# A state-space core worked by feature chunk, four pairs of groups side by side in TensorE's array, in place of pair by pair with zero padding

## The chip, the cores and the metric

The kernel runs on one core of a Trainium2 chip. The metric is the device time of one execution in microseconds. A core has TensorE (matrix products, with a queue of its own for weight loads), VectorE, ScalarE, GpSimd and SyncE (which issues the DMAs); in profile rows they are PE and PEld, DVE, ACT, POOL and SP. They run side by side, each in the order of its own queue, and wait for one another by semaphores.

## The reference

The reference is a stack of layers on a sequence of 256 tokens with 1024 features: in the first block a short convolution, a state-space mixer, an RWKV mixer and another convolution, each followed by a gate and a layer norm; a second block with attention and feed-forward layers follows. The change lies in the state-space mixer:

```python
def s5_mixer(x, w_in, lam_re, lam_im, log_dt, b_re, b_im, c_re, c_im, d_skip, w_glu, b_glu, w_out):
    u, z = jnp.split(x @ w_in, 2, axis=-1)
    ug = u.astype(f32).reshape(bsz, seqlen, SSM_GROUPS, SSM_GROUP)
    ...
    a_bar = jnp.exp(lam * dt)
    b_bar = ((a_bar - 1.0) / lam)[..., None] * b_mat
    bu = jnp.einsum("blgh,gph->blgp", ug, b_bar)
    a_seq = jnp.broadcast_to(a_bar, bu.shape)
    states = lax.associative_scan(_ssm_combine, (a_seq, bu), axis=1)[1]
    y = jnp.einsum("blgp,ghp->blgh", states, c_mat).real + d_skip.astype(f32).reshape(SSM_GROUPS, SSM_GROUP) * ug
    y = jax.nn.gelu(y.reshape(bsz, seqlen, D_INNER).astype(x.dtype))
    y = y * jax.nn.sigmoid(y @ w_glu + b_glu)
    return (y * jax.nn.silu(z)) @ w_out
```

There are 64 groups of 16 features, each with 64 complex states. A chunk is 128 features, so there are 8 chunks of 8 groups.

## The kernel before, in words

Activations lie feature-major: 8 chunks of 128 partitions by 256 tokens. Most weights are split into two halves (`whi` on ScalarE, line 599, `wlo` on VectorE, line 600) and multiplied in three passes; `ssm_in`, the mixer's input projection, is used as plain fp32. An fp32 matmul shows as two rows of the trace.

The order of work is chosen when the program is written out: generators hand out instructions, a planner estimates when each engine is done (`Model`, `Engine`, `TensorE`), and `weave` and `par` emit the generator that can go on first. A side iterator `ada` (the second block's modulation) is woven in at a set pace: per column tile one 512 KB load of `in_ada` and two VectorE products, the `junk` rows of line 1354. The helpers record every operation, so that VectorE and ScalarE instructions have line 402 and matmuls line 431.

`ssm_prep` (818 to 924) makes, during the first layer, the matrices: `bT` for the input product, `ca`, `cm` and `cn` for the output product, `gm` for the direct term of even steps, `rho` and `f2` (size and phase of the recurrence). Two time steps go at a time, so a sequence of 256 becomes two halves of 128. `ple_norm` (778 to 816) ends the first layer with a norm, whose `rsqrt` is a chain of VectorE and ScalarE steps (`tc` rows) before the eight `x` writes from which the projection starts.

`ssm` (926 to 1036): `project` makes the 16 column tiles of the projection (`u` and the gate `sz`). Beside it `pairs(j)` runs for 32 pairs of groups, three at a time. A pair has 32 features and 128 states. Its steps:

- ScalarE copies the pair's 32 rows of `u` into its place in `um`, a buffer that is zero elsewhere;
- the phases: two ScalarE steps, one VectorE step, sine, absolute value, sine, all of 128x128;
- the input product bu: eight 128x128 matmuls (K 128 by way of the zeros) into a `ca` bank;
- VectorE rotates the bank by the phases (`m1`, `m2`, `w`), scans twice along time, and rotates back;
- the output product y: nine matmuls with 32 output columns into 32 rows of a `cb` bank that four pairs share; after the fourth pair VectorE adds the skip term into `y`.

Then come the activation of `y`, the gated product (`ssm_glu`) and `ssm_out`. PSUM banks: three for projections (`mm`), one for sums (`st`), two each of `ca` and `cb`.

Of the kernel before, what the change touches and what calls it, by code (L numbers as in the profile page):

```python
# [86 lines left out]
def constants():  # L87
# [172 lines left out]
# ---------------------------------------------------------------- the program  # L260
# [4 lines left out]
class Stream:  # L265
    """A generator of instructions. It yields a request (array name, block, K chunks, columns) for a weight
    block, which it is sent, or a float where TensorE needs what the other engines have been given to do (Until: a time)."""
# [22 lines left out]
    def keeps(self):  # L290
        """the other stream will want the block too"""
# [29 lines left out]
class Model:  # L321
    """An estimate of when the data of tiles is there, by which the order of instructions is chosen"""
# [29 lines left out]
    def alloc(self, tile, key, bufs):  # L352
        """the tile takes the place of the one `bufs` before it"""
# [7 lines left out]
class Engine:  # L361
    """nc.vector or nc.scalar, with an estimate of when its instructions end: each starts in the first gap that is long
    enough once its operands are there"""
# [17 lines left out]
    def any_time(self, dur):  # L381
        """work whose operands come early"""
# [24 lines left out]
class TensorE:  # L407
    """nc.tensor, with an estimate of the time that its instructions take"""
# [13 lines left out]
    def matmul(self, out, lhsT, rhs, start, stop):  # L422
# [3 lines left out]
        elif m > 64:  # L426
            dur = max(n, 128) / 600.0
# [10 lines left out]
class Net:  # L438
# [45 lines left out]
    def slot(self, i, shape, name, dt=F32):  # L484
        """the i-th of 14 pieces of 8 KB per partition"""
# [9 lines left out]
    def big(self, name):  # L495
        """a piece of 9 KB"""
# [21 lines left out]
    def act(self, out, in_, func, **kw):  # L518
        """an activation; keeps track of the table set that it leaves"""
# [10 lines left out]
    # ---- order of emission  # L530
# [3 lines left out]
    def weave(self, streams, until=None):  # L534
        """emits the streams' instructions, the first that can go on, until the condition or all are done"""
# [51 lines left out]
    # ---- weights: fp32 blocks from DRAM, each split into two float32r parts whose sum it is  # L587
# [22 lines left out]
    def mm3(self, out, w, x, m=0, k0=0, start=True, stop=True):  # L610
        """out += w[:, :, column tile m]^T x[:, k0:] over the K chunks; w, x: (hi, lo) pairs, or float32 both."""
# [14 lines left out]
    def mm3g(self, out, w, x, m=0):  # L626
        """generator: mm3 in pieces, between which others' instructions may go"""
# [1319 lines left out]
```

## Time and profile before

| | us |
|---|---|
| runs | 2926.54, 2930.72, 2931.11 (median 2930.72) |
| span of the profiled execution | 2931.2 |
| PE busy | 2814.3 (96%) |
| DVE busy | 2142.3 (73%) |
| ACT busy | 1631.4 (56%) |
| state-space core, first projection to last y | 185.4 to 357.1 |

The span's row by engine is an average over stages with different limits; the core's own stretch is read by windows, in which busy times of the engines, the granted clock of TensorE (1.00 is 2.4 GHz, 0.50 is 1.2 GHz) and DMA share stand for one stretch. Busy times of PE rows overlap, since matmuls are pipelined; so the distance from start to start is read from rows "xN", which join N like instructions: first start, time from the first start to the last end.

### The profile page before, as it was taken

The page shows a single profiled execution, that of the slowest core. Times are in us where ns is not written, and L with a number is a line of the kernel's source. Part 1 is how long each engine was busy: PE and PEld are TensorE (multiplying, and loading weights), DVE is VectorE, ACT ScalarE, POOL GpSimd, SP SyncE. Part 2 cuts the span into 40 slices and gives each one's busy share as a digit, 9 for nine tenths or more (in the row PEclk, how much of TensorE's full clock was granted, in tenths as well). Part 3 has the DMA queues.
Part 4 walks back from the last instruction along what each step waited for, and adds up shares of the span by engine and source line. Part 5 has one row for each costly group of instructions (what it writes and reads, how often), then busy time and mean ns, then how long its engine had stood idle before and what let it go on. Part 6 is the DMA issues. An engine that isn't in the chain of part 4 may idle for free.

```text
span 2931.2 us, 58792 instructions
## 1 busy us (share of the span) xinstructions
PE 2814.3 (96%) x23798; PEld 2652.5 (90%) x23798; DVE 2142.3 (73%) x4116; ACT 1631.4 (56%) x3069; POOL 16.6 (1%) x42
## 2 busy tenths in 40 slices
PE   8989998899999999999999999999999999999999
PEld 8977788787999999998999978999999999996999
DVE  8876777666678788898898887877855336676655
ACT  5644556766646464778566766544522224466443
POOL 0000000000000000000000000000000000000000
PEclk9989998999999999999999999999999999999999
DMA  7632353200466666666675644666544323221554
GB/s 266 216 130 94 100 185 123 81 23 33 140 213 203 215 201 221 205 194 190 196 224 182 194 155 129 208 223 212 181 144 125 100 82 102 92 87 57 160 182 142
DMA packets 129296, 454.89 MB, mean 155 GB/s; under 512 B 14336, under 2 KB 18688, under 8 KB 128384
## 3 DMA queue, kind: packets, MB, share of 16 engines
q1 hardware_dynamic: 129024, 451.13, 48.3%
q8 instruction: 187, 3.06, 0.4%
q14 instruction: 85, 0.70, 0.1%
HBM read 450.02 MB, written 1.05 MB: 154 GB/s over the span
## 4 chain that ended last, share of the span: by engine, by line
PE 68%; DVE 14%; DMA 8%; ACT 6%; issue 4%; SPq 0%; DVEq 0%; ACTq 0%
PE ps_mm L431 56%; DMA w<-in_ada_dram 7%; PE ps_ca L431 5%; PE ps_cb L431 5%; DVE wlo L600 5%; DVE junk L1354 3%; ACT whi L599 2%; DVE tc L402 1%; PE ps_st L431 1%; PE ps_cb L435 1%; ACT L402 1%; ACT rw_b L402 1%; ACT tc L402 1%; DVE h_lo L402 1%; DMA w<-in_ffn_in_dram 1%
## 5 line engine op out<-in xcount | busy, mean ns | idle before, releaser
L599 ACT ACTIVATE whi<-w 128x1024 fp32r<-128x1024 f32 (+1 forms) x687 | 715.9, 1044 | 731.1 <-PE ps_mm L431 474.1
L600 DVE TENSOR_TENSOR wlo<-w,whi 128x1024 fp32r<-128x1024 f32 (+1 forms) x687 | 826.3, 1204 | 240.7 <-ACT whi L599 238.8
L431 PE MATMUL ps_mm<-h_hi,whi 128*128 128x256 f32 x3024 | 868.0, 289 | 6.1 <-ACT h_hi L402 4.4
L431 PE MATMUL ps_mm<-h_lo,whi 128*128 128x256 f32 x3024 | 856.0, 284 | 2.5 <-DVE h_lo L402 2.4
L431 PE MATMUL ps_mm<-h_hi,wlo 128*128 128x256 f32 x3024 | 853.2, 283 | 3.1 <-DVE wlo L600 3.0
L431 PEld LDWEIGHTS ps_mm<-h_hi,whi 128*128 128x128 f32 x3024 | 569.7, 189 | 15.8 <-ACT h_hi L402 6.3
L431 PEld LDWEIGHTS ps_mm<-h_lo,whi 128*128 128x128 f32 x3024 | 570.2, 189 | 8.7 <-DVE h_lo L402 3.7
L431 PEld LDWEIGHTS ps_mm<-h_hi,wlo 128*128 128x128 f32 x3024 | 570.9, 189 | 7.4 <-DVE wlo L600 4.9
L1354 DVE SCALAR_TENSOR_TENSOR junk<-w,cond 128x1024 bf16<-128x1024 f32 x288 | 351.9, 1222 | 125.9 <-DMA w<-in_ada_dram 124.8
L431 PE MATMUL ps_mm<-d_hi,whi 128*128 128x256 f32 x1232 | 353.4, 287 | 0.9 <-DVE ctx L402 0.4
L431 PE MATMUL ps_mm<-d_hi,wlo 128*128 128x256 f32 x1232 | 348.5, 283 | 3.6 <-DVE wlo L600 3.6
L431 PE MATMUL ps_mm<-d_lo,whi 128*128 128x256 f32 x1232 | 349.6, 284 | 0.0
L431 PEld LDWEIGHTS ps_mm<-d_hi,wlo 128*128 128x128 f32 x1232 | 233.2, 189 | 4.9 <-DVE wlo L600 4.7
L431 PEld LDWEIGHTS ps_mm<-d_hi,whi 128*128 128x128 f32 x1232 | 232.4, 189 | 4.0 <-issue 2.6
L431 PEld LDWEIGHTS ps_mm<-d_lo,whi 128*128 128x128 f32 x1232 | 232.4, 189 | 2.7 <-issue 1.6
L402 DVE TENSOR_TENSOR td<-td,ps_mm 128x256 f32<-128x256 f32 x154 | 64.5, 419 | 82.3 <-PE ps_mm L431 78.8
L402 ACT ACTIVATE d_hi<-td 128x256 fp32r<-128x256 f32 x154 | 63.0, 409 | 79.2 <-DVE td L402 78.4
L402 ACT ACT_TABLE_LOAD x81 | 103.9, 1283 | 2.5 <-PEq L1938 0.7
L431 PE MATMUL ps_mm<-x_hi,whi 128*128 128x256 f32 x256 | 73.6, 287 | 12.4 <-ACT whi L599 12.4
L402 ACT ACTIVATE tc<-tc 128x256 f32<-128x256 f32 x182 | 75.2, 413 | 6.0 <-DVE tc L402 3.1
L402 ACT ACTIVATE td<-ps_mm 128x256 f32<-128x256 f32 x154 | 57.1, 373 | 33.5 <-PE ps_mm L431 33.1
L431 PE MATMUL ps_mm<-xs_hi,whi 128*128 128x256 f32 x256 | 72.7, 284 | 2.7 <-ACT whi L599 1.6
(459 smaller groups left out, 5466.2 us busy)
## 6 DMA issues: line engine op xcount, KB each, us to landing
w<-in_ffn_in_dram SPq DMA_DIRECT2D x268, 512.0 KB, 4.0
w<-in_ada_dram SPq DMA_DIRECT2D x144, 512.0 KB, 4.3
w<-in_ffn_out_dram SPq DMA_DIRECT2D x96, 512.0 KB, 4.1
w<-in_conv_in_dram SPq DMA_DIRECT2D x64, 512.0 KB, 4.5
w<-in_ffn_out_dram SPq DMA_DIRECT2D x48, 384.0 KB, 3.5
w<-in_ab_in_dram SPq DMA_DIRECT2D x34, 512.0 KB, 4.4
w<-in_ple_gate_dram SPq DMA_DIRECT2D x32, 512.0 KB, 4.4
w<-in_conv_out_dram SPq DMA_DIRECT2D x16, 512.0 KB, 4.6
```

What stands on the lines that cost most here:

```text
L402: return f(**kw)
L431: self.t.matmul(out, lhsT=lhsT, rhs=rhs, start=start, stop=stop)
L435: self.t.transpose(out, in_, ident)
L599: nc.scalar.activation(out=hi[:, :n], in_=w[:, :n], func=AF.Copy)
L600: nc.vector.tensor_tensor(out=lo[:, :n], in0=w[:, :n], in1=hi[:, :n].bitcast(F32), op=ALU.subtract)
L1354: nc.vector.scalar_tensor_tensor(out=self.junk, in0=w, scalar=1.0, in1=cb[:, s], op0=ALU.mult, op1=ALU.mult, accum_out=m[:, t, s:s + 1])
```

## The change

The core works by chunk of four pairs, two chunks at a time, each with its own two slots of 8 KB (0 and 1, or 6 and 7).

- bu: instead of 128 rows with zeros, each pair's 32 rows are the contraction, so that four pairs lie in four row quarters of the array; the four results go to four banks (`ca`, `cb`, `ca`, `cb`), from which ScalarE copies them to `w`. `um`, its memset and its 32 copies go; one copy per chunk orders even and odd steps (`uc`).
- y: the four pairs' matmuls with 32 columns each are written next to each other, in four column quarters, into one `st` bank. The direct term's matrix `gm` is now masked to the pairs' blocks (`bd32`, a constant of 128 more columns), by a VectorE multiply in place of the ScalarE copy.
- VectorE and ScalarE steps run over four pairs at once: the phases on 128x512, rotations on 128x1024, sums on 128x512; scans stay 128x128.
- The planner prices such matmuls at a quarter (`share=4`).

```diff
+    c.add("bd32", np.kron(np.eye(4), np.ones((32, 32))))
...
-    def matmul(self, out, lhsT, rhs, start, stop):
+    def matmul(self, out, lhsT, rhs, start, stop, share=1):
...
-        elif m > 64:
-            dur = max(n, 128) / 600.0
+        elif m > 64 or share > 1:
+            dur = max(n, 128) / 600.0 / share
...
-                    A.activation(out=merge(gm[:, 4 * h:4 * h + 4]), in_=ps, func=AF.Copy)
+                    tt(gm[:, 4 * h:4 * h + 4], ps.rearrange("p (c n) -> p c n", c=4), self.c("bd32").unsqueeze(1).to_broadcast([128, 4, 128]), MUL)
...
-        um = self.slot(6, [2, 2, 4, N], "um")
-        nc.gpsimd.memset(um, 0.0)
...
-        sets = [t1_[:, :1024], t1_[:, 1024:], t11[:, 1024:]]
-        free = list(range(3))
+        sets = [tuple(self.slot(k, [2048], f"ssm_m{k}") for k in ks) for ks in ((0, 1), (6, 7))]
+        free = list(range(2))
...
-        def pairs(j):
+        def group(c):
...
-            A.activation(out=uc[rows, :, i], in_=halves(u[rows, c]), func=AF.Copy)
-            v, kk = m2[:, 0], m2[:, 1]
-            A.activation(out=v, in_=tsh, func=AF.Identity, scale=f2[:, j:j + 1])
+            uc = two(self.tmp("ta"))
+            A.activation(out=uc, in_=halves(u[:, c]), func=AF.Copy)
+            for i in range(4):
+                A.activation(out=v[:, i], in_=tsh, func=AF.Identity, scale=f2[:, 4 * c + i:4 * c + i + 1])
             A.activation(out=kk, in_=v, func=AF.Identity, bias=self.fixed[MAGIC])
             V.scalar_tensor_tensor(out=v, in0=kk, scalar=MAGIC, in1=v, op0=SUB, op1=SUB)
-            self.act(cs[:, 1], v, AF.Sin, scale=-TWO_PI)
+            self.act(si, v, AF.Sin, scale=-TWO_PI)
             A.activation(out=v, in_=v, func=AF.Abs)
-            self.act(cs[:, 0], v, AF.Sin, scale=-TWO_PI, bias=half_pi)
+            self.act(co, v, AF.Sin, scale=-TWO_PI, bias=half_pi)
...
-            b = two(self.ps("ca")[:, :S])
+            ps = [self.ps(("ca", "cb")[i % 2])[:, :S] for i in range(4)]
             for q in range(2):
                 for r in range(2):
-                    T.matmul(b[:, q], lhsT=bT[1 - r][:, q, c], rhs=uc[:, r, i], start=r == 0, stop=r == 1)
-            tt(m1, b, co, MUL)
-            tt(m2, b, si, MUL)
...
+                    for i, l in enumerate(lanes):
+                        T.matmul(two(ps[i])[:, q], lhsT=bT[1 - r][l, q, c], rhs=uc[l, r], start=r == 0, stop=r == 1, share=4)
+            for i in range(4):
+                A.activation(out=w[:, i], in_=two(ps[i]), func=AF.Copy)
+            tt(m1, w, both(co), MUL)
+            tt(m2, w, both(si), MUL)
+            tt(w[:, :, 0], m1[:, :, 0], m2[:, :, 1], ADD)
+            tt(w[:, :, 1], m2[:, :, 0], m1[:, :, 1], SUB)
+            for i in range(4):
+                for q in range(2):
+                    x_ = w[:, i, q]
+                    V.tensor_tensor_scan(out=x_, data0=rho[:, 4 * c + i:4 * c + i + 1].to_broadcast([128, N]), data1=x_, initial=0.0, op0=MUL, op1=ADD)
+            tt(m1, w, both(co), MUL)
+            tt(m2, w, both(si), MUL)
             yield 4.0
-            if c not in yps:
-                yps[c] = self.ps("cb")
...
+            yp = two(self.ps("st")[:, :S])
+            for i in range(4):
+                T.matmul(yp[lanes[i], 0], lhsT=gm[:, c, lanes[i]], rhs=uc[:, 0], start=True, stop=False, share=4)
             for r, cc in ((0, ca), (1, cm)):
                 n = N - 1 + r
...
+                for k in range(4):
+                    for i in range(4):
+                        j = 4 * c + i
...
+                        T.matmul(yp[lanes[i], r, N - n:], lhsT=l_, rhs=m_[:, :n], start=r == 1 and k == 0, stop=k == 3, share=4)
             free.append(q_)
...
-        yield from self.par((pairs(j) for j in range(32)), 3, project())
+        yield from self.par((group(c) for c in range(NCH)), 2, project())
```

The change moves instructions on every engine inside the core; before it and behind the start of the gated product the order is the old one. Three places:

ScalarE at the end of the first layer's norm, from the squares (`sq`) to the writes of `x`, before (`tc` are the steps of the inverse root):

```order
L402 ACTIVATE sq<-r 128x256 x8
L393 ACT_TABLE_LOAD
L402 ACTIVATE tc<-ps_st,fixed_64 128x256
L402 ACTIVATE tc<-tc 128x256 x2
L402 ACTIVATE x<-r,pr 128x256 x8
```

The same place after (`ssm_m_2152` and `ssm_m_2153` are the slots of chunk 0: phases, then sine and cosine):

```order
L394 ACT_TABLE_LOAD
L403 ACT_TABLE_LOAD
L403 ACTIVATE ssm_m_2153<-ssm_m_2152 128x512
L403 ACT_TABLE_LOAD
L403 ACTIVATE tc<-ps_st,fixed_64 128x256
L403 ACTIVATE ssm_m_2152<-ssm_m_2152 128x512
L403 ACT_TABLE_LOAD
L403 ACTIVATE tc<-tc 128x256
L403 ACT_TABLE_LOAD
L403 ACTIVATE ssm_m_2153<-ssm_m_2152,fixed_72 128x512
L403 ACTIVATE tc<-tc 128x256
L403 ACTIVATE x<-r,pr 128x256 x8
```

Chunk 0's sine, absolute value and cosine stand among the norm's three steps, with four table loads more. On VectorE at the same place, after, from the last step of the squares' sum to the scaling of `r` (`junk` rows are the modulation's, with the number of their weight tile):

```order
L403 TENSOR_TENSOR sq_2083<-sq_2083 128x256
L1360 SCALAR_TENSOR_TENSOR junk_101,mod_63<-w_2172,cond0_157 128x1024
L403 SCALAR_TENSOR_TENSOR ssm_m0_2152<-ssm_m0_2152 128x512
L1360 SCALAR_TENSOR_TENSOR junk_101,mod_63<-w_2172,cond0_157 128x1024
L1360 SCALAR_TENSOR_TENSOR junk_101,mod_63<-w_2199,cond0_157 128x1024 x2
L403 SCALAR_TENSOR_TENSOR tc_2110<-ps_st_2105,tc_2110 128x256
L1360 SCALAR_TENSOR_TENSOR junk_101,mod_63<-w_2226,cond0_157 128x1024
L403 SCALAR_TENSOR_TENSOR tc_2109<-tc_2110,tc_2109 128x256
L1360 SCALAR_TENSOR_TENSOR junk_101,mod_63<-w_2226,cond0_157 128x1024
L403 SCALAR_TENSOR_TENSOR r_1415<-r_1415,pr_58,tc_2109 128x256 x8
```

Before, two `junk` rows stand there ahead of the first `tc` row, and none between it and `r`.

TensorE inside the core, before (one piece: a part of a projection tile, one pair's y in the column quarter of its rows):

```order
L431 MATMUL ps_mm<-x,w 128x256 x4
L431 MATMUL ps_cb<-um,ssm_s_159 32x128
L431 MATMUL ps_cb<-ssm_s_159,ssm_s_204 32x127 x3
L431 MATMUL ps_cb<-ssm_s_159,cn 32x127
L431 MATMUL ps_cb<-ssm_s_159,ssm_s_203 32x128 x3
L431 MATMUL ps_cb<-ssm_s_159,cn 32x128
```

And after, at chunk 0's y:

```order
L433 MATMUL ps_mm<-x,w 128x256 x20
L433 MATMUL ps_st<-ta,ssm_s_159 32x128 x4
L433 MATMUL ps_st<-ssm_m_2152,ssm_s_204 32x127 x12
L433 MATMUL ps_st<-ssm_m_2152,cn 32x127 x4
L433 MATMUL ps_st<-ssm_m_2152,ssm_s_203 32x128 x12
L433 MATMUL ps_st<-ssm_m_2152,cn 32x128 x4
L433 MATMUL ps_mm<-x,w 128x256 x12
```

A y is now 36 matmuls in one piece, and neighbours in a row lie in different column quarters.

ScalarE between chunks 2 and 3, after (`2152`, `2153` hold chunk 2, `2154`, `2155` chunk 3; `fixed_70` adds the rounding number, `fixed_72` makes the second sine of the phases a cosine):

```order
L403 ACTIVATE ssm_m_2153<-ssm_m_2152,fixed_72 128x512
L403 ACTIVATE u<-ps_mm 128x256
L403 ACTIVATE ta<-u 128x256
L403 ACTIVATE ssm_m_2154<-cond_157,f_161 128x128 x4
L403 ACTIVATE ssm_m_2154<-ssm_m_2154,fixed_70 128x512
L403 ACTIVATE ssm_m_2155<-ssm_m_2154 128x512
L403 ACTIVATE ssm_m_2154<-ssm_m_2154 128x512
L403 ACTIVATE ssm_m_2153<-ps_ca 128x256
L403 ACTIVATE ssm_m_2153<-ps_cb 128x256
```

Chunk 2's evictions from `ps_ca` and `ps_cb` stand behind chunk 3's phases and its first sine; before, nothing was evicted there, since VectorE read the `ca` banks itself.

## Rows read from the trace of the kernel before

**Rows 1.** Stretches: length, busy us (rows) of each engine, clock, DMA.

```profile
core 0: us, PE busy (x) PEld busy (x) DVE busy (x) ACT busy (x) POOL busy (x), PEclk, DMA share, GB/s
173.00:190.00 17.00, 9.05 (x21) 6.23 (x21) 14.42 (x34) 8.97 (x20) 0.00 (x0) 0.50 0.19 62
190.00:344.00 154.00, 152.97 (x1043) 124.00 (x1042) 107.38 (x323) 70.73 (x194) 0.00 (x0) 1.00 0.29 93
347.10:354.00 6.90, 5.60 (x27) 4.50 (x27) 4.82 (x14) 4.24 (x11) 1.82 (x4) 0.51 0.36 112
354.00:430.00 76.00, 76.00 (x628) 75.07 (x627) 57.68 (x100) 43.73 (x82) 2.70 (x6) 1.00 0.59 183
```

**Rows 2.** The chain of waits from 191 to 357 us, by line.

```profile
by line: PE ps_cb L431 38.0%; PE ps_mm L431 35.9%; PE ps_ca L431 19.0%; DMA w<-in_ssm_glu_dram 2.8%; DVE ssm_s L402 1.9%; ACT ssm_s L402 0.8%; issue 0.6%; ACT whi L599 0.6%; DVE y L402 0.3%; DVE mod L402 0.1%; DVE wlo L600 0.0%
```

**Rows 3.** Groups from 191 to 362 us: busy, mean ns | idle, releaser.

```profile
L431 PE MATMUL ps_mm<-x,w 128*128 128x256 f32 x243 | 62.3, 390 | 0.0
L431 PEld LDWEIGHTS ps_cb<-ssm_s,ssm_s 128*32 128x32 f32 x384 | 39.2, 111 | 13.6 <-DVE ssm_s L402 8.1 <-issue 3.0 <-ACT whi L599 0.2
L431 PE MATMUL ps_ca<-um,bT 128*128 128x128 f32 x256 | 37.0, 286 | 1.0 <-DVE ssm_s L402 1.0
L431 PE MATMUL ps_cb<-ssm_s,ssm_s 128*32 128x127 f32 x192 | 30.5, 281 | 4.0 <-DVE ssm_s L402 3.9
...
L1354 DVE SCALAR_TENSOR_TENSOR junk<-w,cond 128x1024 bf16<-128x1024 f32 x20 | 24.3, 1217 | 0.6 <-DMA w<-in_ada_dram 0.6
...
L402 ACT ACTIVATE ssm_s<-ssm_s 128x128 f32<-128x128 f32 x58 | 17.2, 301 | 4.3 <-DVE ssm_s L402 3.5
...
L402 ACT ACTIVATE um<-u 32x256 f32<-32x256 f32 x32 | 13.8, 432 | 2.0 <-PE ps_cb L431 1.3
...
L600 DVE TENSOR_TENSOR wlo<-w,whi 128x1024 fp32r<-128x1024 f32 x4 | 4.8, 1217 | 0.0
...
L402 ACT ACTIVATE u<-ps_mm 128x256 f32<-128x256 f32 x8 | 3.0, 377 | 13.1 <-PE ps_mm L431 13.1
```

**Rows 4.** TensorE's timeline: start us, length us, runs of like matmuls.

```profile
202.13 0.82 PE L431 MATMUL ps_cb<-ssm_s,ssm_s 128*32 128x128 f32 x6
...
207.10 2.05 PE L431 MATMUL ps_ca<-um,bT 128*128 128x128 f32 x16
208.99 5.35 PE L431 MATMUL ps_mm<-x,w 128*128 128x256 f32 x24
```

**Rows 5.** TensorE's timeline in the RWKV heads and the attention.

```profile
587.35 0.68 PE L431 MATMUL ps_cb<-rw_b 128*64 128x64 f32 x14
...
1324.06 1.08 PE L431 MATMUL ps_mm<-pt,kava 128*64 128x256 f32 x8
```

**Rows 6.** VectorE's timeline: runs of like instructions inside the core.

```profile
261.98 0.75 DVE L402 TENSOR_TENSOR ssm_s<-ssm_s 128x256 f32<-128x256 f32 x2
...
263.58 0.74 DVE L402 TENSOR_TENSOR_SCAN ssm_s<-rho,ssm_s 128x128 f32<-128x128 f32 x2
...
341.89 2.36 DVE L600 TENSOR_TENSOR wlo<-w,whi 128x1024 fp32r<-128x1024 f32 x2
```

**Rows 7.** Timeline of the norm's end, all engines.

```profile
179.16 1.28 ACT L393 ACT_TABLE_LOAD   x1
...
183.45 0.42 DVE L402 SCALAR_TENSOR_TENSOR tc<-ps_st,tc 128x256 f32<-128x256 f32 x1 [2.01 <-ACT tc L402]
...
185.45 7.73 PE L431 MATMUL ps_mm<-x,w 128*128 128x256 f32 x24 [3.44 <-ACT x L402]
```

**Rows 8.** Timeline of the core's end, TensorE and VectorE.

```profile
348.40 1.48 PE L431 MATMUL ps_cb<-ssm_s,ssm_s 128*32 128x127 f32 x6 [3.95 <-DVE ssm_s L402]
...
351.94 1.01 PE L431 MATMUL ps_mm<-ys_hi,whi 128*128 128x256 f32 x3
...
356.61 0.48 DVE L402 SCALAR_TENSOR_TENSOR y<-u,pr,ps_cb 128x256 f32<-128x256 f32 x1 [1.23 <-PE ps_cb L431]
```

More of the change, by code (lines that the diff above doesn't have):

```diff
@@ L822, in ssm_prep @@
         N = S // 2
[L823 removed]
+        tsh = self.second[:, 2 * D:2 * D + N + 128]
         self.consts("ssm", tsh)
@@ L960, in ssm @@
             A.activation(out=cn[:, r], in_=cc[:, 1], func=AF.Copy, scale=-1.0)
[L961 to L964 removed]
+        sets = [tuple(self.slot(k, [2048], f"ssm_m{k}") for k in ks) for ks in ((0, 1), (6, 7))]
+        free = list(range(2))
         halves = lambda t: t.rearrange("p (t r) -> p r t", r=2)
         two = lambda t: t.rearrange("p (q t) -> p q t", q=2)
[L968 to L969 removed]
+        lanes = [slice(32 * i, 32 * i + 32) for i in range(4)]
+        def group(c):
             while c not in came:
@@ L972, in pairs @@
             q_ = free.pop(0)
-            m1, m2, cs, w = (two(sets[q_][:, 256 * q:256 * q + 256]) for q in range(4))
-            rows = slice(32 * i, 32 * i + 32)
-            uc = um[:, c % 2]
-            A.activation(out=uc[rows, :, i], in_=halves(u[rows, c]), func=AF.Copy)
-            v, kk = m2[:, 0], m2[:, 1]
-            A.activation(out=v, in_=tsh, func=AF.Identity, scale=f2[:, j:j + 1])
+            a, b = sets[q_]
+            m1, m2, w = (t.rearrange("p (i q t) -> p i q t", i=4, q=2) for t in (a[:, :1024], a[:, 1024:], b[:, :1024]))
@@ L980, in pairs @@
+            co, si = (b[:, 1024 + 512 * k:1536 + 512 * k].rearrange("p (i t) -> p i t", i=4) for k in range(2))
+            v, kk = (a[:, 1024 + 512 * k:1536 + 512 * k].rearrange("p (i t) -> p i t", i=4) for k in range(2))
+            uc = two(self.tmp("ta"))
+            A.activation(out=uc, in_=halves(u[:, c]), func=AF.Copy)
+            for i in range(4):
+                A.activation(out=v[:, i], in_=tsh, func=AF.Identity, scale=f2[:, 4 * c + i:4 * c + i + 1])
             A.activation(out=kk, in_=v, func=AF.Identity, bias=self.fixed[MAGIC])
@@ L981, in pairs @@
             V.scalar_tensor_tensor(out=v, in0=kk, scalar=MAGIC, in1=v, op0=SUB, op1=SUB)
-            self.act(cs[:, 1], v, AF.Sin, scale=-TWO_PI)
+            self.act(si, v, AF.Sin, scale=-TWO_PI)
             A.activation(out=v, in_=v, func=AF.Abs)
-            self.act(cs[:, 0], v, AF.Sin, scale=-TWO_PI, bias=half_pi)
-            co, si = (cs[:, q:q + 1].to_broadcast([128, 2, N]) for q in range(2))
+            self.act(co, v, AF.Sin, scale=-TWO_PI, bias=half_pi)
+            both = lambda t: t.unsqueeze(2).to_broadcast([128, t.shape[1], 2, N])
@@ L986, in pairs @@
             yield 2.0
-            b = two(self.ps("ca")[:, :S])
+            ps = [self.ps(("ca", "cb")[i % 2])[:, :S] for i in range(4)]
             for q in range(2):
                 for r in range(2):
-                    T.matmul(b[:, q], lhsT=bT[1 - r][:, q, c], rhs=uc[:, r, i], start=r == 0, stop=r == 1)
-            tt(m1, b, co, MUL)
-            tt(m2, b, si, MUL)
-            tt(w[:, 0], m1[:, 0], m2[:, 1], ADD)
-            tt(w[:, 1], m2[:, 0], m1[:, 1], SUB)
-            for q in range(2):
-                V.tensor_tensor_scan(out=w[:, q], data0=rho[:, j:j + 1].to_broadcast([128, N]), data1=w[:, q], initial=0.0, op0=MUL, op1=ADD)
@@ L999, in pairs @@
+            for i in range(4):
[4 more added lines that the diff above has]
+            tt(m2, w, both(si), MUL)
             yield 4.0
-            if c not in yps:
-                yps[c] = self.ps("cb")
-            yp = two(yps[c][:, :S])
-            T.matmul(yp[rows, 0], lhsT=gm[:, c, rows], rhs=uc[:, 0, i], start=True, stop=False)
+            yp = two(self.ps("st")[:, :S])
@@ L1004, in pairs @@
+            for i in range(4):
+                T.matmul(yp[lanes[i], 0], lhsT=gm[:, c, lanes[i]], rhs=uc[:, 0], start=True, stop=False, share=4)
             for r, cc in ((0, ca), (1, cm)):
                 n = N - 1 + r
-                for k, (l_, m_) in enumerate(((cc[:, 0, j], m1[:, 0]), (cc[:, 0, j], m2[:, 1]), (cc[:, 1, j], m2[:, 0]), (cn[:, r, j], m1[:, 1]))):
-                    T.matmul(yp[rows, r, N - n:], lhsT=l_, rhs=m_[:, :n], start=r == 1 and k == 0, stop=k == 3)
+                for k in range(4):
+                    for i in range(4):
+                        j = 4 * c + i
+                        l_, m_ = ((cc[:, 0, j], m1[:, i, 0]), (cc[:, 0, j], m2[:, i, 1]), (cc[:, 1, j], m2[:, i, 0]), (cn[:, r, j], m1[:, i, 1]))[k]
+                        T.matmul(yp[lanes[i], r, N - n:], lhsT=l_, rhs=m_[:, :n], start=r == 1 and k == 0, stop=k == 3, share=4)
@@ L1008, in pairs @@
             free.append(q_)
-            left[c] -= 1
-            if left[c] == 0:
-                V.scalar_tensor_tensor(out=halves(y[:, c]), in0=halves(u[:, c]), scalar=self.p("ssm_d", c), in1=two(yps.pop(c)[:, :S]), op0=MUL, op1=ADD)
+            V.scalar_tensor_tensor(out=halves(y[:, c]), in0=halves(u[:, c]), scalar=self.p("ssm_d", c), in1=yp, op0=MUL, op1=ADD)
         self.fine = FINE & 1
-        yield from self.par((pairs(j) for j in range(32)), 3, project())
+        yield from self.par((group(c) for c in range(NCH)), 2, project())
```

8 lines of the change are left out of this document (1 added, 7 removed).

## Prediction

> **What bounds the kernel now.** I read the stretches first, because the order of work differs only between the end of the first layer's norm and the gated product (GLU) behind the state-space core; elsewhere each engine has its old row order, so the forecast is a shift of everything behind the core. From 190 to 344 us TensorE is busy 152.97 of 154 us at the full clock, VectorE 107.38, ScalarE 70.73 [rows 1]; the chain of waits runs over TensorE there (38.0, 35.9 and 19.0%) [rows 2]. TensorE's work falls into three parts, by start-to-start distance in runs of one kind [rows 3, 4]: 256 rows of projection (243 recorded) at (5.35-0.39)/23 = 0.216 us, 55 us; 256 rows of input product (bu) at (2.05-0.29)/15 = 0.117, 30 us (another run gives 0.122); 576 rows of output product (y; six groups of `ps_cb`, the largest shown) at (0.82-0.27)/5 = 0.109, 63 us. That is 148 us, the stage. Two rows make one fp32 matmul.
>
> **The change, part by part.** TensorE keeps its matmul count: a chunk has 32 bu rows and 72 y rows. Before, they cost 32 x 0.122 = 3.9 and 72 x 0.109 = 7.85 us a chunk. Now four neighbours in the order use four different quarters of the array. The trace never shows four. It shows two: 14 rows of 128*64 tiles in 0.68 us (0.068 us each after the first), and eight rows 128x256 in 1.08 us where a row by itself takes 0.216 every time [rows 4, 5]: pairs run nearly as one. From two to four is an extrapolation; bounds for a chunk are 2.0 + 1.0 us (all four as one) and 7.85 + 3.9 (none). I take 2.1 + 1.0, as the rows that are nearest show nearly full overlap, and keep the partial case as a rival. TensorE's need then falls from 148 to 55 + 8 x 3.1 = 80 us, and **another engine sets the end**.
>
> The Trainium skill ("TensorE: Matmul & The Clock Gate", Part 3: Packing small matmuls — row/col tiling) says that a weight load overlaps running matmuls only in another row group, which speaks against the y part, whose four column tiles use all rows. Here the column-tile loads, 111 ns each, hide behind matmuls on the same rows, at 0.109 us a row [rows 3, 4]; by the row y is 2.1 us a chunk, by the rule 36 x 0.111 + 2.1 = 6.1, an estimate, and the sum would be near 2903.
>
> VectorE per chunk: four 128x1024 at 1.14 (2.36-1.22, the split), two 128x512 at 0.65 (twice the 128x256's 0.33), eight scans at 0.33 [rows 6]: 4.6+1.3+2.6 = **8.6 us**, plus y 0.5 and the phase step 0.65. This is hardly less than before: the same elements in fewer instructions.
>
> ScalarE: the 32 copies into the padded buffer (13.8 us) go, one of 128x256 per chunk (0.4) comes; the bu result is now evicted, four of 128x256 at 0.38 per chunk [rows 3]. The phase chain becomes 128x512 at about 0.6 (128x128 0.30, 128x256 0.38, carried on). TensorE hid ScalarE before; now it stands in the path.
>
> *Start of the core.* Chunk 0's sines can only be written once the old tenants of its slots are done, so they fall into the norm's ScalarE chain, where Sin, Ln and Exp alternate: five table loads instead of one, each 1.28 [rows 7]. By the new order: squares end 179.1; two loads to 181.7; sin 182.3; load, Ln 184.1; abs 184.7; load, Exp 186.4; load 187.7; sin 188.3; Square 188.7. VectorE's step after it moves from 183.45 [rows 7] to 188.7. Two modulation products (1.2 each [rows 3]) now stand between it and the x writes: first projection at 185.45 + 5.2 + 2.4 less rounding = **192.9, 7.5 us late**. Then three projection tiles (48 rows) precede bu. The clock was 1.2 GHz until 190.1, 4.65 us after the first matmul [rows 1, 7]; the same again gives 11 rows at 0.43 and 37 at 0.216: 205.6. bu 1.0, and the last evictions: VectorE starts chunk 0 at **207.9**.
>
> *A cycle of two chunks* (two sets of buffers), from the start t of chunk c's block: block c ends t+8.6; block c+1 with one modulation product between, t+18.4; product 19.6; y(c) 20.1; phase step of c+2 20.75; ScalarE sin, abs, sin 22.6; copies u and uc 23.4. Chunk c+3's phases (4 x 0.3 + 0.6) 25.2: ScalarE takes them ahead of c+2's evictions. VectorE's step 25.85; sin, abs 27.05; evictions 4 x 0.38: 28.6. So **28.6**, of which VectorE works 22: it waits about 6 us per cycle for a ScalarE queue in which c+2's evictions stand behind c+3's sine. TensorE's y(c+1) ends at 20.5 and bu(c+2) at 24.4, both in cover; its 3.25 projection tiles and four products take 18 us. Cycle 3 has eight modulation products and a weight split in VectorE's order, part of them in the wait: 31.5 by the same steps. Tail: two blocks 17.2, a product and a split 2.4, y(c6) 0.5, the last y 2.1 + 0.5: 22.7.
>
> *Sum:* 207.9 + 2 x 28.6 + 31.5 + 22.7 = 319.3, where before the last y ends at 357.1 (356.61 + 0.48) [rows 8]: 37.8 earlier. Behind it the GLU is dense on TensorE (76.00 of 76 busy) [rows 1], so the shift passes on whole, less what is lost at the border: GLU rows that before ran ahead of the last y (from 351.94 on), and the low clock when TensorE comes out of the tail's wait, as at 348.40 to 354 [rows 1, 8]: 2.5. For a y on the path at half clock 1.0. Saving 34.3.
>
> Edits at nothing: the mask multiply (two 128x512 on VectorE instead of ScalarE copies), 64 KB more constants and the memset dropped from GpSimd lie in the first layer, under projections; if that cover is gone they cost 2 x 0.65. Two modulation products move behind the core, under the dense GLU.
>
> The sum is against the profiled span, 2931.2, which is 0.5 above the median 2930.7. 2931.2 - 34.3 = 2896.9; I say **2896**. About 0.2% (5.9 us) is what a measurement can tell from no change.
>
> **Rivals.** *A, tiles overlap only by twos* (bu serial 3.9, y 3.9). For: only pairs are shown. Against: nothing shows a limit at two. (Whatever makes y 4 to 6 us, weight loads among it, is this case.) TensorE's need per cycle is then 11.4 + 4 x 3.9 = 27, level with 28.6, so its queue slips 1 to 1.5 us per cycle; with the first bu +2.9 and the last y +1.8 that is about +8: **2904**. *B, the clock is down about half the time.* For: TensorE idles some 10 us per cycle, and the clock was at 1.2 GHz after the pauses before 185.45 and 348.40 [rows 1, 7, 8]. Against: the projection tiles lie between. Half of the 18 us doubled adds 9 us of work, of which the wait behind in-order projections lets about 5 show per cycle: four times 5 is +20: **2916**. *C, the slower end: the clock stays down through the whole core.* TensorE per cycle 4 x 7 + 2 x (4.1 + 2.0) = 40 us, over VectorE's 28.6, and TensorE is the bound again: 192.9 + 13 tiles and products, 160 us, + the last block 11 = 364, 7 later than before, and 3 to 4 at the border: **2942**. It decides once a cycle passes some 37 us, (357 - 207.9)/4. Against: before, the clock came back after some 5 us of work [rows 1, 7, 8]. The Trainium skill ("TensorE: Matmul & The Clock Gate", HAM oscillation — how this bites in real kernels) describes this: bursts parted by waits run at the low clock each time. By it the time would be C's or B's; the trace has it after single pauses only. *D, no overlap at all:* 148 us of TensorE plus 7.5 of late start, **2939**; the rows with pairs exclude it for columns.
>
> **How the numbers follow.** Forecast 0.66 (2880 to 2908), A 0.11, B 0.12, C 0.06, D 0.02, the rest (a start that costs more, an order that I read wrong) 0.03 on either side. The low end 2880: if evictions don't wait for the next sine, a cycle is 25 (3.6 less, four times). The range 2880 to 2918 takes in the forecast, A and B's centre: 0.82 or so. Faster 0.91; slower 0.07 (C, D's upper part); within 0.2%: 0.02.
>
> **What would show it.** In the changed profile: the first `ssm_in` matmul near 193 and four or five table loads ahead of it (start); four bu or y matmuls starting within some 20 ns, bu groups every 0.12 us (if by twos, A); VectorE's 128x1024 pairs 28 to 31 us apart per cycle with waits on ScalarE, not on TensorE (bound); a granted clock near 1.0 through the core (if 0.5 to 0.8, B or C); the last y near 319; the GLU as dense as before. I am wrong if TensorE ends the waits in the core, if the start is not late, or if work behind the GLU doesn't move as one.

## The result and the profile after

The changed kernel takes 2893.44 us (median of four runs, 2889.6 to 2898.43), the kernel before 2930.91 beside it: a ratio of 0.9878, interval 0.9862 to 0.9893, so 37.5 us less. The forecast was 2896. The profiled execution spans 2890.5 us, 40.7 less than the one of before. Its device time is 2892.28, so an execution takes 1.8 us more than its span; by that it lies 1.2 us under the median, and the profiled one of before (2931.2 + 1.8) lies 2.1 above. So stretches are compared with each other first and with the medians only in sum.

The stretches of the changed kernel, core 0 (length, busy us and rows of each engine, clock, DMA share, GB/s), answer to [rows 1]:

```profile
184.00:195.00 11.00, 0.30 (x1) 0.00 (x0) 6.61 (x15) 7.39 (x12) 0.00 (x0) 0.50 0.32 95
195.00:200.00 5.00, 4.89 (x12) 3.91 (x13) 2.28 (x6) 2.85 (x8) 0.00 (x0) 0.50 0.36 105
210.00:237.00 27.00, 25.32 (x294) 21.47 (x292) 21.62 (x39) 11.77 (x27) 0.00 (x0) 1.00 0.34 116
239.00:265.00 26.00, 21.83 (x263) 17.97 (x263) 23.62 (x40) 11.19 (x28) 0.00 (x0) 0.93 0.35 103
267.00:295.00 28.00, 21.82 (x266) 18.32 (x258) 27.83 (x49) 10.39 (x25) 0.00 (x0) 0.88 0.41 132
300.00:320.00 20.00, 9.53 (x141) 6.69 (x142) 19.05 (x38) 8.61 (x20) 3.80 (x8) 0.51 0.19 54
320.00:393.00 73.00, 73.00 (x606) 72.69 (x606) 58.13 (x100) 42.33 (x75) 1.60 (x3) 1.00 0.63 200
```

TensorE, busy all the time in the core before, now waits in every cycle (1.7, 4.2 and 6.2 us in the three stretches from 210 to 295), and VectorE's busy share rises from 0.80 in the first to 0.99 in the third. By these shares alone TensorE would still look like the bound of the first cycle (25.32 of 27 us). The chain of waits through the core (210 to 319 us), which answers to [rows 2], decides: TensorE's lines fall from 93% to 10.7%.

```profile
by line: DVE ssm_m L403 61.0%; DVE junk L1360 12.5%; PE ps_st L433 7.5%; ACT ssm_m L403 7.3%; issue 4.5%; PE ps_mm L433 2.1%; DVE wlo L602 2.1%; DVE y L403 1.8%; PE ps_ca L433 0.9%; ACT sz L403 0.4%; PE ps_cb L433 0.2%
```

TensorE's timeline at chunk 0's bu (five rows of 32) and at its y (72 rows in five runs); start, length:

```profile
208.14 0.37 PE L433 MATMUL ps_ca<-ta,bT 32*128 32x128 f32 x1
208.15 0.37 PE L433 MATMUL ps_cb<-ta,bT 32*128 32x128 f32 x1
208.16 0.37 PE L433 MATMUL ps_ca<-ta,bT 32*128 32x128 f32 x1
208.16 0.37 PE L433 MATMUL ps_cb<-ta,bT 32*128 32x128 f32 x1
208.36 0.27 PE L433 MATMUL ps_ca<-ta,bT 32*128 32x128 f32 x1
...
221.10 0.43 PE L433 MATMUL ps_st<-ta,ssm_s 128*32 128x128 f32 x8
221.35 0.83 PE L433 MATMUL ps_st<-ssm_m,ssm_s 128*32 128x127 f32 x24
222.00 0.40 PE L433 MATMUL ps_st<-ssm_m,cn 128*32 128x127 f32 x8
222.21 0.84 PE L433 MATMUL ps_st<-ssm_m,ssm_s 128*32 128x128 f32 x24
222.87 0.40 PE L433 MATMUL ps_st<-ssm_m,cn 128*32 128x128 f32 x8
```

Four bu rows start within 20 ns of one another; all 32 end at 209.32, 1.2 us after the first began. The 72 rows of y take 2.17 us (221.10 to 223.27), as one column quarter did before with 18 rows [rows 4]. The four tiles run nearly as one.

ScalarE's table loads at the norm's end, then VectorE's first step behind them and the first projection, against [rows 7]:

```profile
181.45 1.28 ACT L394 ACT_TABLE_LOAD   x1
182.74 1.28 ACT L403 ACT_TABLE_LOAD   x1
...
184.68 1.28 ACT L403 ACT_TABLE_LOAD   x1
...
186.99 1.28 ACT L403 ACT_TABLE_LOAD   x1
...
188.72 1.28 ACT L403 ACT_TABLE_LOAD   x1
...
191.07 0.42 DVE L403 SCALAR_TENSOR_TENSOR tc<-ps_st,tc 128x256 f32<-128x256 f32 x1 [4.33 <-ACT tc L403]
...
195.11 13.11 PE L433 MATMUL ps_mm<-x,w 128*128 128x256 f32 x48 [10.80 <-ACT x L403]
```

VectorE's timeline at the first rotation of each pair of chunks and at the last y, against [rows 8]:

```profile
210.58 3.69 DVE L403 TENSOR_TENSOR ssm_m<-ssm_m 128x1024 f32<-128x1024 f32 x4 [13.29 <-ACT ssm_m L403]
...
238.87 3.69 DVE L403 TENSOR_TENSOR ssm_m<-ssm_m 128x1024 f32<-128x1024 f32 x4 [2.45 <-ACT ssm_m L403]
...
266.67 3.69 DVE L403 TENSOR_TENSOR ssm_m<-ssm_m 128x1024 f32<-128x1024 f32 x4 [3.47 <-ACT ssm_m L403]
...
297.29 2.36 DVE L403 TENSOR_TENSOR ssm_m<-ssm_m 128x1024 f32<-128x1024 f32 x2
...
319.88 0.48 DVE L403 SCALAR_TENSOR_TENSOR y<-u,pr,ps_st 128x256 f32<-128x256 f32 x1 [0.94 <-PE ps_st L433]
```

From one first rotation to the next, the cycles are 28.3, 27.8 and 30.6 us; the tail, from 297.29 to the end of the last y, is 23.1. Each of the three cycles begins behind ScalarE. What ScalarE does before the second one starts at 238.87:

```profile
233.68 1.26 ACT L403 ACTIVATE ssm_m<-cond,f 128x128 f32<-128x128 f32 x4
...
236.45 1.29 ACT L403 ACTIVATE ssm_m<-ssm_m 128x512 f32<-128x512 f32 x2 [0.76 <-DVE ssm_m L403]
237.65 0.37 ACT L403 ACTIVATE ssm_m<-ps_ca 128x256 f32<-128x256 f32 x1
```

Chunk 2's bu ends at 233.60, but its first eviction starts at 237.65, behind chunk 3's phases and first sine: the order that "The change" shows. In the chain in order of time (start, length), y of chunk 1 ends a wait at full clock, y of chunk 3 and the last product at low clock, and the GLU is dense. The last row is the dense run of the kernel before:

```profile
230.33 2.17 PE ps_st L433 x72
...
257.48 3.43 PE ps_st L433 x72
...
316.64 3.16 PE ps_st L433 x56
319.80 73.63 PE ps_mm L433 x608
...
356.57 72.64 PE ps_mm L431 x600
```

### The profile page after: what moved, and what is told of

It is laid out like the page before. It is cut to its first block, busy times and chain, and to the rows that moved or that the text cites. A ratio compares the mean times of both kernels' runs of the same rounds, so it can differ in the third digit from the quotient of the medians.

```text
span 2890.5 us, 58487 instructions
## 1 busy us (share of the span) xinstructions
PE 2749.0 (95%) x23798; PEld 2601.8 (90%) x23798; DVE 2129.7 (74%) x3950; ACT 1613.4 (56%) x2982; POOL 14.8 (1%) x41
## 4 chain that ended last, share of the span: by engine, by line
PE 72%; DVE 13%; ACT 7%; DMA 5%; issue 3%; SPq 0%; ACTq 0%; DVEq 0%
PE ps_mm L433 62%; PE ps_ca L433 5%; DMA w<-in_ada_dram 4%; DVE wlo L602 3%; DVE junk L1360 3%; PE ps_cb L433 2%; DVE ssm_m L403 2%; ACT whi L601 2%; PE ps_st L433 2%; DVE tc L403 1%; PE ps_cb L437 1%; ACT L403 1%; ACT rw_b L403 1%; ACT tc L403 1%; DVE h_lo L403 1%
```

## The experiments

Theory 1 is the prediction's: tiles side by side free TensorE, and VectorE with ScalarE's queue takes its place. Theory 2: fewer, wider instructions on VectorE and ScalarE and fewer waits make the gain. All edits are to the changed kernel. "Last y" is the end of VectorE's last y step; every time is a median of four or more runs beside 2930 to 2931 for the kernel before.

### The same matmuls in the order of pairs

```diff
-            for q in range(2):
-                for r in range(2):
-                    for i, l in enumerate(lanes):
+            for i, l in enumerate(lanes):
+                for q in range(2):
+                    for r in range(2):
                         T.matmul(two(ps[i])[:, q], lhsT=bT[1 - r][l, q, c], rhs=uc[l, r], ...)
...
+            for i in range(4):
+                ...
+                for r, cc in ((0, ca), (1, cm)):
-                for k in range(4):
-                    for i in range(4):
+                    for k in range(4):
```

The first hunk alone is the bu run, the second alone the y run; the first run has both.

> The changed kernel with the same matmuls in another order: bu pair by pair (quarter of rows by quarter) and y pair by pair (quarter of columns by quarter), so that neighbours no longer lie in different quarters. Everything else (wide phases, evictions, one chunk at a time) stays. Theory 1 (the gain is tiles of the array working side by side): TensorE is the bound again, per two chunks 11.4 us of projection and 2 x (7.85 + 3.9) of products = 35 us, four times, from 195; core end near 355, time 2925 to 2940. Theory 2 (the gain is fewer and wider VectorE and ScalarE instructions, with fewer waits between engines): 2893 to 2905.

> Only y in the order of pairs, bu side by side. Theory 1: y of the second chunk ends 18.4 + 7.85 us into a cycle in place of 20.5, so the next chunk's phases start later on ScalarE: a cycle is 31.5 to 32 us in place of 28, three times, and the last y costs 5.8 more: 2905 to 2912, with y at 7.8 us a chunk in the trace. Theory 2, or a y that ran no faster side by side: 2893 to 2897.

> Only bu in the order of pairs, y side by side. Theory 1: bu takes 3.9 us a chunk in place of 1.0; the first one delays the core by 2.9, the later ones end near where the evictions begin, up to 1 us each: 2896 to 2902. Theory 2, or row tiles that ran no faster side by side: 2893 to 2895. A bu that costs its whole 2.9 us eight times would give 2916.

Measured: both 2922.75 (2916.22 to 2930.84, ten runs; ratio to before 0.9974, 0.9961 to 0.9987), y alone 2912.64, bu alone 2895.74. In this order: the stretch of the first run, one y of it in the chain in order of time, the chains through the core (210 to 330 us) of the first, of y alone and of bu alone:

```profile
215.00:290.00 75.00, 75.00 (x586) 67.53 (x585) 48.41 (x84) 28.20 (x64) 0.00 (x0) 1.00 0.27 85
...
222.84 6.73 PE ps_st L433 x72
...
by line: PE ps_st L433 38.7%; PE ps_mm L433 36.9%; DVE ssm_m L403 7.9%; PE ps_cb L433 6.0%; PE ps_ca L433 5.5%; DVE wlo L602 2.0%; issue 1.3%; DVE junk L1359 1.2%; ACT ssm_m L403 0.6%; DVEq L602 0.0%; ACTq L403 0.0%
...
by line: PE ps_st L433 39.6%; PE ps_mm L433 31.9%; DVE ssm_m L403 16.6%; ACT ssm_m L403 3.2%; PE ps_ca L433 2.9%; DVE junk L1359 2.1%; issue 1.8%; PE ps_cb L433 1.0%; DVE wlo L602 0.9%; ACT ys_hi L403 0.4%; ACTq L403 0.1%; DVEq L1359 0.0%
...
by line: DVE ssm_m L403 58.7%; DVE junk L1360 9.8%; ACT ssm_m L403 9.8%; PE ps_mm L433 8.3%; issue 4.5%; PE ps_st L433 2.7%; DVE wlo L602 2.4%; DVE y L403 1.6%; PE ps_cb L433 1.0%; PE ps_ca L433 0.5%; ACT ta L403 0.4%; ACT u L403 0.3%; DVE 
```

With the same matmuls in another order TensorE is again busy all the time (75.00 of 75) and 29 of the 37.5 us are gone. The other 8 stay, and theory 2 may have them: this run's last y ends at 341.9, where before it ended at 357.1. No run takes the wider instructions apart from what moved with them.

Serial y alone costs 19.2 us over the changed kernel, since it puts TensorE in 75% of the chain by itself. Serial bu alone stays in cover (2.3 us, within noise of nothing). The other 8 of the 29 us appear only with both.

Serial y takes 6.73 us a chunk and not the 7.85 that was expected, and serial bu 2.8 (211.19 to 214.01) and not 3.9, because at the border of two pairs neighbours still lie in different quarters and overlap (rows start 0.03 us apart there, 0.11 within a pair). So the last y of the first run came 13 us before the expected 355 and its time undercuts its range by 2. Serial y lies above its range (2905 to 2912) by under 1 us, serial bu just under its own (2896 to 2902).

### Chunk 0's sines out of the norm

```diff
-                A.activation(out=v[:, i], in_=tsh, func=AF.Identity, scale=f2[:, 4 * c + i:4 * c + i + 1])
+                ph = A.activation(out=v[:, i], in_=tsh, func=AF.Identity, scale=f2[:, 4 * c + i:4 * c + i + 1])
+                if c == 0 and i == 0:
+                    self.tc.keep_in_program_order(ph)
```

> Chunk 0's phase chain pinned behind the copy of its u, so that no sine stands among the norm's Ln, Exp and Square steps on ScalarE: one table load there in place of five. Theory 1 (the late start is the table loads and what moved between the norm's steps): the first projection matmul starts near 188 in place of 195.1 and the core and all behind it shift: 2885 to 2889. Rival: the sines then hold up chunk 0's evictions, or the projection waits for its weights, and VectorE's first rotation stays near 210.6: 2892 to 2895.

Measured: 2887.57 (2884.93 to 2888.18), ratio 0.9855 (0.984 to 0.987): 5.9 us below the changed kernel. ScalarE's load and steps at the norm's end, and the first projection:

```profile
183.13 1.28 ACT L394 ACT_TABLE_LOAD   x1
...
189.86 12.31 PE L433 MATMUL ps_mm<-x,w 128*128 128x256 f32 x48 [3.88 <-ACT x L403]
```

The norm has one load in place of five; the squares ended 1.7 us later here. From the first table load to the first matmul it is 6.7 us, against 13.7 in the changed kernel and 6.3 before [rows 7]. So the change put 7.4 us there, forecast 7.5, and this run takes 6.9 of them back, with the load order and the two modulation products that moved with it.

### Modulation held through the core

```diff
+        self.hold += 1
         yield from self.par((group(c) for c in range(NCH)), 2, project())
+        self.hold -= 1
```

The second of these runs has one line more, `self.next = self.now()`, which lets the modulation go on at its old pace in place of catching up.

> The modulation's side iterator is held from the core's beginning to its end, so that its 20 products and loads near the core are written later, beside the dense GLU or a catch-up at the core's end. Theory 1 (VectorE is in the path of the core, so each product between blocks costs its 1.2 us): the first two cycles fall from 28 to about 26, the start by 2.4 us for the two products among the norm's steps: 2883 to 2889. Rival (the wait for ScalarE sets the cycle and the products lie in it, or the second block waits for the modulation later): 2891 to 2896.

> The changed kernel with the modulation held through the core, as in the earlier run with it held (2897.9), but without the catch-up behind it: its clock starts anew at the core's end, at its old pace. Theory (the held run's 10 us of earlier core end were lost to the crowd of 512 KB modulation loads beside the GLU's own weights): the GLU runs dense again and the gain stays, 2884 to 2890. Rival (the modulation has to be made up somewhere, and costs as much wherever that is, or the second block waits for it): 2894 to 2900.

Measured: 2897.92 (2895.95 to 2901.34) and 2894.61 (2891.11 to 2895.73). The second lies in its rival's range, the first above even that (2891 to 2896). The last y came 10 and 11 us earlier (310.2 and 309.2 against 320.4), so VectorE's products do cost their time in the core; but the modulation is owed. In the first run ten of the core's 16 products still stand in it, all in its last 40 us; its first two cycles hold none, and last 25.7 and 26.6 us with VectorE still waiting for ScalarE (2.45 and 3.20 us). The held run's chain from 310 to 390 us, beside the GLU:

```profile
by line: PE ps_mm L433 19.9%; DMA w<-in_ssm_out_dram 11.9%; DVE wlo L602 11.3%; issue 11.0%; DVE junk L1362 7.1%; ACT whi L601 6.8%; DMA w<-in_ssm_glu_dram 6.4%; DMA w<-in_rwkv_r_dram 5.9%; DMA w<-in_ple_gate_dram 5.2%; DVE ta L403 4.3%; DV
```

In the changed kernel the GLU's stretch (320 to 393 us) is one piece of TensorE. Here five `in_ada` loads go between the other weights on SyncE's queue from 319 to 354 us, and the chain waits for those weights, 4 to 5 us each time. Without the catch-up the GLU is short again (table below), and the same time is lost behind it; where is not shown.

### The phases ahead, and ScalarE's order

The phases get a scratch and four pairs of buffers (slot 2 and the free halves), so that chunk c + 2's can be written while chunk c is worked; `phases(c)` is the old code:

```diff
+            if c < 2:
+                phases(c)
...
             tt(m2, w, both(si), MUL)
+            if c + 2 < NCH:
+                phases(c + 2)
             yield 4.0
```

The next run adds to it the pin of chunk 0's phases and the held modulation. The third instead pins each later chunk's first phase step to its place in program order, that is behind the present chunk's evictions, and gives chunk 0 the slots that come free first:

```diff
-        sets = [... for ks in ((0, 1), (6, 7))]
+        sets = [... for ks in ((6, 7), (0, 1))]
...
+                if c > 0:
+                    self.tc.keep_in_program_order(ph)
```

The fourth is the third with the modulation held, without catch-up.

> The phases (sine and cosine) get buffers of their own, four deep, and each chunk's are written two chunks ahead, so that no eviction stands behind a later chunk's sine. With it the planner also moves most modulation products out of the core. Theory 1 (VectorE waits some 6 us per cycle for ScalarE's queue): a cycle falls from 28 to 20 to 23 us, VectorE's own 17.2 + 2.3 or TensorE's 18, core end near 300: 2868 to 2876. Rival A (TensorE's order of projection tiles is the wait, not ScalarE): cycles stay at 26 to 28, 2883 to 2893, of which the moved products alone explain the gain as in the run with the modulation held.

> Phases ahead, chunk 0's phases pinned behind its u, and the modulation held, together. Theory 1: the three gains lie in different stretches, except that the products are counted once: 2860 to 2869. Rival (pinned phases of chunks 0 and 1 share one scratch buffer and now delay the first blocks by what the start gains): 2868 to 2876.

> Phases in buffers of their own as in the run with phases ahead, and in addition a fixed place on ScalarE: each later chunk's phases stand behind the present chunk's evictions, chunk 1's behind its u, and chunk 0 uses the slots that come free first, so that the norm's steps have one table load. Modulation where the planner puts it. Theory 1 (two waits for ScalarE's order, the norm's table loads and the evictions behind later phases, are what VectorE loses in the core): first projection near 189, chunks 9.7 to 10.5 us apart, last y near 292 (319.9 with the change alone, 306.7 with phases ahead). The time depends on what the GLU gives back: with as much as the other runs with a short core, 2878 to 2884. Rival (the chunks' distance is set by TensorE's order of projection tiles): last y 300 to 307, 2884 to 2890.

> The fixed ScalarE order of phases and evictions, with the modulation held through the core and no catch-up behind it. Theory (as for both parts): last y near 285, the gain stays through the GLU: 2864 to 2876. Rival (modulation costs as much wherever it is made up): 2878 to 2886.

Measured: 2889.80, 2881.97, **2870.98** (2866.65 to 2874.6; ratio to before 0.9796, 0.978 to 0.9811) and 2870.83. The buffers alone gave little (3.6 us; the theory had 2868 to 2876), because the order stayed: chunk 2's bu ended at 226.8, but ScalarE first waited for VectorE to free a buffer for chunk 5's sines, then wrote these and chunk 6's phases, and only then evicted chunk 2. The time fell into rival A's range (2883 to 2893), but not for its reason, TensorE's order. ScalarE's timeline there, and VectorE's, with a phase step and the rotation:

```profile
227.22 0.63 ACT L403 ACTIVATE ssm_m<-ssm_s 128x512 f32<-128x512 f32 x1 [4.34 <-DVE ssm_m L403]
...
229.76 1.27 ACT L403 ACTIVATE ssm_s<-cond,f 128x128 f32<-128x128 f32 x4
...
231.69 0.36 ACT L403 ACTIVATE ssm_m<-ps_ca 128x256 f32<-128x256 f32 x1
...
231.82 0.69 DVE L403 SCALAR_TENSOR_TENSOR ssm_s<-ssm_s 128x512 f32<-128x512 f32 x1 [4.24 <-ACT ssm_s L403]
232.91 2.36 DVE L403 TENSOR_TENSOR ssm_m<-ssm_m,ssm_c 128x1024 f32<-128x1024 f32 x2 [0.40 <-ACT ssm_m L403]
```

With the order fixed the wait is gone: y steps come 9.4 us apart (222.61, 232.01, 241.43, 250.83, 260.24), VectorE's own work for a chunk. No modulation product lies in that stretch, nor in the first two cycles of the held run (25.7 and 26.6 us) and of the buffers alone (23.3 and 25.2). So a cycle of 18.8 us shows what the order is worth: 4 to 6 us a cycle over the buffers alone, 7 to 8 over neither. The stretches of the core and of the GLU of that run, and the chains through both:

```profile
205.00:285.00 80.00, 71.57 (x970) 60.41 (x969) 79.72 (x139) 43.31 (x106) 1.66 (x4) 0.95 0.31 100
287.00:370.00 83.00, 78.31 (x621) 76.79 (x622) 73.06 (x129) 46.38 (x82) 1.94 (x4) 0.98 0.72 231
...
by line: DVE ssm_m L403 84.0%; DVE junk L1373 7.1%; DVE ssm_s L403 4.5%; DVE y L403 3.0%; DVE wlo L602 1.4%; issue 0.5%; DVE mod L403 0.2%; DVE ga L403 0.2%
...
by line: PE ps_mm L433 37.4%; DMA w<-in_ssm_out_dram 18.2%; DVE wlo L602 12.7%; DMA w<-in_ple_gate_dram 6.4%; issue 5.5%; DVE junk L1373 5.0%; ACT whi L601 4.4%; DVE ta L403 3.1%; DVE g_lo L403 1.7%; DVE rs_lo L403 1.4%; DVE ys_lo L403 1.0%
```

VectorE is busy 79.72 of 80 us. Of 33.5 us that the last y comes earlier, 22.5 reach the end: the GLU now waits for weights. From the last y to the next norm 35 loads of 512 KB are issued, where the changed kernel has 29. Four of the six more are modulation that the planner moved out of the core here too, and two are the GLU's own, which the changed kernel issues within its longer core.

The run did better than its range (2878 to 2884). The fourth lies in its own (2864 to 2876), but holding the modulation gave nothing over the third (0.15 us). The run with everything missed both of its ranges (2860 to 2876 together): chunk 0 and 1 shared one scratch and the second block came late (y at 205.95, then 230.66).

Where each execution spent its time, from its own profile:

| run | first projection | last y ends | to the next norm | from there to the end | span |
|---|---|---|---|---|---|
| the change | 195.1 | 320.4 | 87.9 | 2482.3 | 2890.5 |
| sines late | 189.9 | 314.0 | 87.8 | 2484.4 | 2886.3 |
| held | 193.5 | 310.2 | 94.3 | 2492.3 | 2896.8 |
| held, no catch-up | 191.7 | 309.2 | 89.4 | 2494.3 | 2892.8 |
| phases ahead | 194.9 | 307.2 | 92.9 | 2484.9 | 2885.0 |
| all three | 183.5 | 289.7 | 97.8 | 2488.6 | 2876.1 |
| order fixed | 188.1 | 286.9 | 96.4 | 2485.8 | 2869.1 |
| order fixed, held | 187.1 | 287.5 | 92.5 | 2487.3 | 2867.3 |

"Next norm" is VectorE's first `tc` step of the norm behind the GLU. The stretch to the next norm is longer in every run in which modulation left the core. The last column varies by execution: in the two runs of the next part, which change nothing behind the core, it is 2491.5 and 2481.0. So only the two held runs, 10 and 12 us above the changed kernel, stand out there, the first barely.

### TensorE kept busy before the first projection

```diff
+        ps = self.ps("ca")
+        for _ in range(14):
+            self.tc.keep_in_program_order(nc.tensor.matmul(ps[:, :S], lhsT=self.c("ident"), rhs=..., start=True, stop=True))
```

The second run has 23 of them.

> Fourteen fp32 matmuls 128x256 of no use in the wait before the first projection (some 10.8 us in which TensorE idles), their result thrown away. Theory (the first projection rows ran at 1.2 GHz because TensorE had idled): granted clock 1.0 from the first projection on, its 48 rows in 10.5 us in place of 13.1, 2890 to 2892. Rival: the clock does not come up, or the added rows end after x is there: 2893 to 2897.

> As the run with 14 matmuls of no use in the wait before the first projection, with 23, since those 14 ended 4 us before x came and the clock was down again. Theory: no pause before the projection, granted clock 1.0 there, its first 48 rows in 10.5 us in place of 13.1 (12.3 with 14), bu of chunk 0 near 205.5 after the same start: 2889 to 2892. Rival: the added rows push the projection back, or the rows take 12 us or more all the same: 2893 to 2897.

Measured: 2894.60 (2893.65 to 2900.11), in the rival's range, and 2889.61 (2887.97 to 2894.93), in the theory's. The stretch 195 to 200 us with 14, then 190 to 200 us and TensorE's rows with 23:

```profile
195.00:200.00 5.00, 5.00 (x17) 4.08 (x16) 1.73 (x5) 2.30 (x6) 0.00 (x0) 0.66 0.22 88
...
190.00:195.00 5.00, 5.00 (x25) 4.39 (x24) 2.68 (x5) 2.27 (x3) 0.00 (x0) 1.00 0.16 65
195.00:200.00 5.00, 5.00 (x25) 4.41 (x24) 3.53 (x10) 3.30 (x8) 0.00 (x0) 1.00 0.34 105
185.34 11.74 PE L966 MATMUL ps_ca<-bT,cs_base 128*128 128x256 f32 x46
196.92 10.52 PE L433 MATMUL ps_mm<-x,w 128*128 128x256 f32 x48
```

Fourteen ended 4 us before x came, and the clock was down again for a part of the first tiles; 23 reached up to them, and 48 projection rows took 10.52 us in place of 13.11. So the low clock there costs 2.6 us, where the sum had 2.4 (11 rows at 0.43 in place of 0.216). The whole time (3.8 lower) agrees, but the spreads overlap.

## Why the prediction was right, point by point

**The start.** Predicted 192.9 for the first projection, measured 195.1. The squares ended at 181.4 and not 179.1: in a stretch of one order in both kernels VectorE waited longer for the modulation's loads. The same point lies between 177.2 and 183.1 in the experiments, so this may be chance; that the change has no part in it is not shown. The five table loads came in the forecast order and cost 7.4 us with their company, forecast 7.5. VectorE's first rotation came 15.5 us after the first projection, forecast 15.0.

**Tiles side by side.** 2.17 us for y and 1.2 for bu, forecast 2.1 and 1.0. That four would run as two did was the extrapolation, and it held; rival A falls by the rows, and D by the first run: in the order of pairs TensorE is the bound again. D's price was too high (2939 against 2922.75): it took 7.85 + 3.9 us a chunk, where the serial order measured 6.73 + 2.8, so 131 us of TensorE and not 148.

The rule that a weight load overlaps matmuls of other row groups only (the Trainium skill, "TensorE: Matmul & The Clock Gate", Part 3: Packing small matmuls — row/col tiling) would make y 6.1 us by the prediction's count of 36 loads. That count was half of what the rows say, a load for each of the 72 rows, so that by the rule it would be 72 x 0.111 + 2.1 = 10.1, an estimate. Here the four column tiles use the same rows and y takes 2.17 with its loads, so the measurement decides against the rule in this form.

**The bound.** Cycles 28.3, 27.8, 30.6 and a tail of 23.1, forecast 28.6, 28.6, 31.5 and 22.7. The term that carries it, about 6 us per cycle in which VectorE waits for evictions behind the next chunk's phases, is shown by its removal: with the phases ahead and ScalarE's order fixed a cycle takes 18.8 us, against 25.7 and 26.6 in the held run, all without modulation products. It was not seen how much of that gain the next stretch gives back.

**The low clock.** 1.0 us was set for a y at half clock in the path; chunk 3's took 3.43 in place of 2.17, and the last product's part behind its wait 3.16, where the sum had 2.1 (both above), so about 2.3. The clock's mean over the middle cycles, 0.93 and 0.88, is neither C nor B: it fell after waits within cycles (0.61 from 257.4 to 261), but was back at 1.00 from 263 on, among projection tiles. In the tail, which has none, it was 0.51.

**The sum.** Last y 320.4, forecast 319.3. That it is so near is in part luck: the first rotation came 2.7 us late, the three cycles were 2.0 short together, the tail 0.4 long. The dense GLU run starts at 319.80 and lasts 73.63, where before it started at 356.57 and lasted 72.64: the shift at its end is 35.8, forecast 34.3. At the border 0.9 us was lost (36.7 of lead at the last y), where 2.5 was set.

Behind it the lead between the two profiled executions grows to 40.7, in an order that both kernels share. Of these 4.9 us, 3.3 are the executions themselves, one 1.2 us under its median and the other 2.1 above. The medians lie 37.5 apart; the 1.7 us between that and 35.8 stay open and are within the spread of the runs. So the forecast was 2.6 us high because its saving, 34.3, was 3.2 too small. That it took 2931.2, a span, for a device time did no harm, since that lies by chance near the median, 2930.91.

Two sums of the prediction are off without weight in it: the 36 loads above, and the chances, which add to 1.03 if 0.03 stands on either side.

## What to carry to other kernels

Matmuls that fill a quarter of the array cost about a third here (y 2.17 us against 6.73, bu 1.2 against 2.8) when the neighbours in the order lie in different quarters; the same matmuls pair by pair gave 29 of 37.5 us back. When that frees TensorE, read the other engines' queues in order: here an eviction behind a later chunk's sine and five table loads in a norm were worth another 22 us, and buffers without a fixed order gave 3.6 of it. And work moved out of a path is owed: ask which transfers it brings into the stretch where it lands.

## What the runs showed that was not expected

The modulation's products cost 1.2 us each in VectorE's path, but moving them won nothing: 10 and 11 us gained in the core by holding them became 4.5 and 1.2 us lost in all (the second within noise), and with the order fixed the time stayed the same. And the GLU, which TensorE bounds in the changed kernel (73 of 73 us busy, DMA share 0.63), waited for `in_ssm_out` in 18.2% of its chain once six more loads fell beside it (DMA share 0.72).
